# The factors of the norms of a two-layer decoder trunk, moved from ScalarE and VectorE to GpSimd

## The chip, the cores and the metric

The kernel runs on one core of a Trainium2 chip. A core has five engines with a queue of instructions each: TensorE (PE: matrix products and transposes; PEld is its loading of weights), VectorE (DVE), ScalarE (ACT: functions by table, and copies with a scale), GpSimd (POOL) and SyncE (SP, which here issues DMAs). They run side by side and wait for each other by semaphores; each runs its own queue in order. The metric is the device time of one launch in microseconds, the median of several runs.

## The reference, cut to what matters

1024 positions of width 1024 pass two layers. Each layer is a token mixer with four heads of cross attention to a memory of 256 rows, one output projection, and a squared-ReLU MLP of width 4096; layer 0 mixes by latent attention, layer 1 by sliding-window attention. Every branch begins with an RMS norm:

```python
def rmsnorm(x, g):
    y = x * rsqrt(mean(x * x, axis=-1) + EPS)      # EPS = 1e-6
    return y * g

mem_n = rmsnorm(mem, mem_norm_g)
for i in range(2):
    hn = rmsnorm(x, attn_norm_g[i])
    mix, q_cross = mixer_i(hn)                     # layer 0 also norms c_q (384) and c_kv (256)
    x = x + concat(mix, cross(q_cross, mem_n)) @ w_o[i]
    x = x + relu(rmsnorm(x, mlp_norm_g[i]) @ w_up[i])**2 @ w_down[i]
return rmsnorm(x, final_norm_g)
```

What matters here is the factor of each norm, one number per position: the inverse root of the mean square plus EPS.

## The kernel before

**Tiling.** Positions lie on the 128 partitions, in 8 row tiles of 128. A factor is thus a column of 128x1 values, and all arithmetic on it is on such columns (128x2 where two norms share one). Matrix products take each fp32 operand as a high and a low part (`split`: ACT writes the high part, L99 or L102, and DVE subtracts it for the low part, L100 or L103) and run three matmuls (`mm3`, or `mm3w` at L117 to L120). An operand that has to stand with its features on the partitions is transposed by PE into PSUM (`psT...`), and `split` from there.

**Order.** The source is written tile by tile, but the order in which each engine gets its instructions is worked out by the scheduler of the tile framework when the program is built, from the dependencies and from how free each engine is by its reckoning. A change of what runs where thus also changes the order on all engines, and each engine then runs its order as it stands.

**The norms.** There are 50 factors, made in two ways.

- `rstd_of` (L166) and `newton` (L180): ACT squares a tile and sums it (`ss`), DVE turns the sum into mean plus EPS (`z`, L177), ACT takes the root (L184), DVE the reciprocal (L185), and four small DVE operations make a Newton step (L186 to L189). It serves the two memory tiles (`mem_T`; the factor is used at L443, and the product `ym` is transposed at L447), the input norm of each row tile in layer 0 (`norm_y`, used at L206, transposed into `psT_a` at L213), and the two norms on each tile's projection (`a_in`, used at L559 and L560): 18 chains.
- `Rstd.get` (from L1153): the same with one operation fewer (z L1154, root L1155, reciprocal L1156, Newton step L1157 to L1159), for the 32 norms on half rows of 512: the norm ahead of the MLP in `wo_phase` (used by ACT at L1230 and DVE at L1231, transposed into `psT_m` at L1241), and those behind the MLP (`Down.norm` and `late_norm`; used at L1740 or L1694, transposed into `psT_b` at L1751; in layer 1 at L1742 straight to the output).

**Stages.** Memory norm and its projections (to 50 us); layer 0's input projection, one tile each 12.6 us (to 150 us); attention; output projection, whose second half also norms (to 550 us); MLP up and down (to 1175 us); layer 1 likewise (output projection to 1510 us), and the last norm, tile by tile behind the last matmuls. In the projection, the input norm of tile t+1 is made while PE multiplies tile t: `psin` are the projection's sums, `psT_a` the transposes of the next tile's normed input, which stand among them in PE's queue, and `psct` those of the normed result. `psu` and `psv` are products of the MLP's up part, behind the last `psT_m`.

POOL does masks, some products in attention (L430, L2004), the scaling of some weights (L1857) and the issue of some DMAs (L1308, L1688, L1733).

Of the kernel before, what the change touches and what calls it, by code (L numbers as in the profile page):

```python
# [13 lines left out]
AF = mybir.ActivationFunctionType  # L14
ALU = mybir.AluOpType
# [5 lines left out]
D = 1024  # L21
# [5 lines left out]
EPS = 1e-6  # L27
# [28 lines left out]
def trunk(  # L56
# [7 lines left out]
    nc = tc.nc  # L64
# [104 lines left out]
    def rstd_of(pl, src_parts, junk):  # L169

        k = len(src_parts)
        small_ct[0] += 1
        ss = pl.tile([P, 2], F32, tag="ss", bufs=4, name=f"ss{small_ct[0]}")
        z = pl.tile([P, 2], F32, tag="zs", bufs=4, name=f"zs{small_ct[0]}")
        for i, (ap, n) in enumerate(src_parts):
            nc.scalar.activation(junk[:, :n], ap, AF.Square, accum_out=ss[:, i : i + 1])
            nc.vector.tensor_scalar(z[:, i : i + 1], ss[:, i : i + 1], 1.0 / n, EPS, ALU.mult, ALU.add)  # L177
        return newton(pl, ss, z[:, :k], k)

    def newton(pl, ss, z, k):  # L180

        rs = pl.tile([P, 2], F32, tag="rs", bufs=4, name=f"rs{small_ct[0]}")
        rk, t = rs[:, :k], ss[:, :k]
        nc.scalar.activation(t, z, AF.Sqrt)  # L184
        nc.vector.reciprocal(rk, t)  # L185
        nc.vector.tensor_tensor(t, rk, rk, ALU.mult)  # L186
        nc.vector.tensor_tensor(t, t, z, ALU.mult)
        nc.vector.tensor_scalar(t, t, -0.5, 1.5, ALU.mult, ALU.add)
        nc.vector.tensor_tensor(rk, rk, t, ALU.mult)  # L189
        return rs  # L190

    def rstd_halves(pl, xt, junk):

        small_ct[0] += 1
        ss = pl.tile([P, 2], F32, tag="ss", bufs=4, name=f"ss{small_ct[0]}")
        for i, c in enumerate((slice(0, 512), slice(512, 1024))):
            nc.scalar.activation(junk[:, c], xt[:, c], AF.Square, accum_out=ss[:, i : i + 1])
        z = pl.tile([P, 2], F32, tag="zs", bufs=4, name=f"zs{small_ct[0]}")[:, 0:1]
        nc.vector.tensor_scalar(z, ss[:, 0:1], ss[:, 1:2], 1.0 / D, ALU.add, ALU.mult)
        nc.vector.tensor_scalar(z, z, EPS, None, ALU.add)  # L200
        return newton(pl, ss, z, 1)

    def norm_y(pl, xt, y):

        rs = rstd_of(pl, [(xt, D)], y)
        nc.vector.tensor_scalar(y, xt, rs[:, 0:1], None, ALU.mult)  # L206
# [934 lines left out]
    class Rstd:  # L1141
# [9 lines left out]

        def get(self):
            ss, z, rk, t = self.st[:, 0:2], self.st[:, 2:3], self.st[:, 3:4], self.st[:, 4:5]  # L1153
            nc.vector.tensor_scalar(z, ss[:, 0:1], ss[:, 1:2], EPS, ALU.add, ALU.add)  # L1154
            nc.scalar.activation(t, z, AF.Sqrt)  # L1155
# [942 lines left out]
```

## Time and profile before

| | |
|---|---|
| median of three runs | 2132.03 us (2131.01 to 2135.06) |
| profiled execution | 2133.53 us |
| its span, first to last instruction | 2131.8 us |
| mean granted clock of TensorE | 0.998 |
| DVE busy | 1473.0 us, 69% |
| ACT busy | 1136.7 us, 53% |
| POOL busy | 160.0 us, 8% |

1.7 us of the profiled execution lie outside its span. How to read the rows: in the list of waits a row names who waited, for which engine and line, and then the us in total, how often, and the longest. A row of a timeline has start and length in us, engine, line, operation, the written and the read tiles, their shapes, and in brackets how long the engine stood idle just before and for whom. A row of one line's view has its count and the least, median and longest duration in ns. A row of groups has count, busy us and mean ns, then the engine's idle time ahead of it.

### The profile page before, as it was taken

The numbers are of one execution on the slowest core, as the hardware profiler recorded it, in microseconds if no ns is written. First come the engines' busy times: TensorE is split into PE (matmuls) and PEld (weight loads), VectorE is DVE, ScalarE is ACT, GpSimd is POOL, SyncE is SP. The second block draws the span as 40 slices with busy tenths as digits, with TensorE's granted clock in tenths as the row PEclk, the third lists the DMA queues.
The fourth block names the chain that finished last, engine by engine and source line by source line (L and its number), as shares of the span: only waits on it lengthen the run. The fifth ranks groups of instructions, "written<-read, shape, count | busy, mean of one in ns | idle before, by whom it ended". The sixth has DMA issues, their size and how long they took to land.

```text
span 2131.8 us, 29050 instructions
## 1 busy us (share of the span) xinstructions
PE 2081.3 (98%) x9928; PEld 1707.1 (80%) x9928; DVE 1473.0 (69%) x2829; ACT 1136.7 (53%) x2440; POOL 160.0 (8%) x224
## 2 busy tenths in 40 slices
PE   6999999999999999999999999999999999999998
PEld 5888787778777788888888888778888778888887
DVE  7555688865887677886557543866977776976565
ACT  5455477766744544444445553976744443444452
POOL 0012100000000000000001241631000000000000
PEclk9999999999999999999999999999999999999999
DMA  7202223443254455954443211142354446944342
GB/s 255 58 10 56 64 61 81 108 138 108 97 171 144 142 163 184 325 191 140 153 115 94 75 31 50 41 124 80 114 163 163 139 134 222 331 157 155 117 120 88
DMA packets 173726, 275.05 MB, mean 129 GB/s; under 512 B 17189, under 2 KB 72970, under 8 KB 173578
## 3 DMA queue, kind: packets, MB, share of 16 engines
q1 hardware_dynamic: 167008, 256.91, 38.1%
q0 software_dynamic: 4016, 13.12, 1.7%
q10 hardware_dynamic: 2554, 3.17, 0.4%
q8 instruction: 78, 1.28, 0.3%
q14 instruction: 70, 0.57, 0.1%
HBM read 183.79 MB, written 76.86 MB: 122 GB/s over the span
## 4 chain that ended last, share of the span: by engine, by line
PE 75%; DMA 9%; DVE 8%; ACT 5%; issue 2%; SPq 0%; POOL 0%; DVEq 0%; ACTq 0%; POOLq 0%
PE psy L1758 5%; PE psy L1760 5%; PE psy L1759 5%; PE psz L1758 4%; PE psz L1760 4%; PE psz L1759 4%; DMA d<-in_mlp_w_up_dram 4%; PE pss L885 4%; PE pso L927 3%; DMA mr<-in_mlp_w_up_dram 3%; PE psu L1423 3%; PE psu L1425 3%; PE psu L1424 3%; PE pswo L110 2%; PE pswo L108 2%; PE pswo L109 2%
## 5 line engine op out<-in xcount | busy, mean ns | idle before, releaser
L1323 ACT ACTIVATE mr<-mr,gcol 128x256 f32<-128x256 f32 (+1 forms) x160 | 67.2, 477 | 85.1 <-DMA mr<-in_mlp_w_up_dram 81.5
L1323 ACT ACTIVATE d<-d,gcol 128x256 f32<-128x256 f32 x128 | 57.8, 500 | 83.4 <-DMA d<-in_mlp_w_up_dram 76.1
L1758 PE MATMUL psy<-g 128*128 128x512 f32 x256 | 99.9, 390 | 0.0
L1759 PE MATMUL psy<-g 128*128 128x512 f32 x256 | 99.6, 389 | 0.0
L1760 PE MATMUL psy<-g 128*128 128x512 f32 x256 | 99.3, 389 | 0.0
L99 ACT ACTIVATE g<-i 128x512 fp32r<-128x512 f32 x79 | 49.6, 628 | 89.0 <-PE psz L1759 46.4
L100 DVE TENSOR_TENSOR g<-i,g 128x512 fp32r<-128x512 f32 x79 | 55.4, 701 | 49.9 <-ACT g L99 49.7
L99 ACT ACTIVATE uh<-i 128x512 fp32r<-128x512 f32 x66 | 41.6, 630 | 85.3 <-PE psy L1759 40.7
L99 ACT ACTIVATE i<-mr 128x512 fp32r<-128x512 f32 x78 | 49.1, 629 | 69.5 <-PE psy L1759 20.6
L906 ACT ACTIVATE p<-pss 128x512 f32<-128x512 f32 x108 | 63.5, 592 | 41.2 <-PE pss L885 41.1
L100 DVE TENSOR_TENSOR pl<-p,ph 128x512 fp32r<-128x512 f32 (+1 forms) x96 | 61.6, 651 | 27.4 <-ACT ph L99 26.9
L760 DVE TENSOR_REDUCE m<-psx 128x1 f32<-128x128 f32 (+5 forms) x96 | 70.2, 748 | 11.0 <-PE psx L756 10.8
L100 DVE TENSOR_TENSOR uh<-i,uh 128x512 fp32r<-128x512 f32 x66 | 45.5, 690 | 45.3 <-ACT uh L99 45.2
L1759 PE MATMUL psz<-g 128*128 128x512 f32 x192 | 74.7, 389 | 0.0
L1760 PE MATMUL psz<-g 128*128 128x512 f32 x192 | 74.7, 389 | 0.0
L1758 PE MATMUL psz<-g 128*128 128x512 f32 x192 | 74.7, 389 | 0.0
L100 DVE TENSOR_TENSOR i<-mr,i 128x512 fp32r<-128x512 f32 x78 | 53.6, 687 | 22.5 <-ACT i L99 22.2
L99 ACT ACTIVATE ph<-p 128x512 fp32r<-128x512 f32 (+1 forms) x96 | 56.4, 599 | 1.3
L1760 PEld LDWEIGHTS psy<-g 128*128 128x128 f32 x256 | 48.1, 188 | 10.0
L1759 PEld LDWEIGHTS psy<-g 128*128 128x128 f32 x256 | 48.1, 188 | 9.9
L1758 PEld LDWEIGHTS psy<-g 128*128 128x128 f32 x256 | 48.1, 188 | 9.8
L1639 DVE TENSOR_TENSOR mqf<-mqq,mqf 128x512 f32<-128x512 f32 x64 | 43.1, 687 | 16.4 <-DMA mqq<-in_mlp_w_down_dram 16.2
(646 smaller groups left out, 6914.2 us busy)
## 6 DMA issues: line engine op xcount, KB each, us to landing
i<-hd SPq DMA_DIRECT2D x154, 256.0 KB
hd<-uh SPq DMA_DIRECT2D x76, 256.0 KB
hd<-ul SPq DMA_DIRECT2D x76, 256.0 KB
mr<-in_mlp_w_up_dram SPq DMA_DIRECT2D x36, 512.0 KB
hd<-x SPq DMA_DIRECT2D x72, 256.0 KB
mr<-hd SPq DMA_DIRECT2D x70, 256.0 KB
d<-in_mlp_w_up_dram SPq DMA_DIRECT2D x32, 512.0 KB
mqq<-in_mlp_w_down_dram SPq DMA_DIRECT2D x32, 512.0 KB
```

Source lines behind the costliest of these rows:

```text
L99: nc.scalar.activation(hi, src, AF.Copy)
L100: nc.vector.tensor_tensor(lo, src, f32(hi), ALU.subtract)
L760: nc.vector.reduce_max(m8s[h][:, i : i + 1], ps[:, c], axis=AX, negate=True)
L885: return lambda: nc.tensor.matmul(o, a, b, skip_group_check=True, **kw)
L927: mms.append(lambda: nc.tensor.matmul(o, a, b, skip_group_check=True, **kw))
L1323: nc.scalar.activation(w[:, k, :], w[:, k, :], AF.Copy, scale=g_mlp[layer][:, k0 + k : k0 + k + 1])
L1423: nc.tensor.matmul(ps, wh[:, k, :], xh[:, k, :], start=p in (1, 2, 5) and k == 0, stop=False, skip_group_check=True)
L1424: nc.tensor.matmul(ps, wh[:, k, :], xl[:, k, :], start=False, stop=False, skip_group_check=True)
L1425: nc.tensor.matmul(ps, wl[:, k, :], xh[:, k, :], start=False, stop=k == 3, skip_group_check=True)
L1758: nc.tensor.matmul(ps, ah[:, j, :], bh, start=p in (1, 5, 2) and k == 0, stop=False, skip_group_check=True)
L1759: nc.tensor.matmul(ps, ah[:, j, :], bl, start=False, stop=False, skip_group_check=True)
L1760: nc.tensor.matmul(ps, al[:, j, :], bh, start=False, stop=k == NP - 1, skip_group_check=True)
```

## The change

All arithmetic on the factors goes to GpSimd. Root and reciprocal become one power with the exponent -0.5, read from a small constant tile; the Newton step follows with four operations (in `Rstd.get` three before). ScalarE still squares and sums, and still applies factors; its Sqrt goes, and with it the loads of the table that Sqrt needs (eight loads of tables in all before, three now). VectorE loses 281 instructions, ScalarE 62, GpSimd gains 309.

```diff
         for i, (ap, n) in enumerate(src_parts):
             nc.scalar.activation(junk[:, :n], ap, AF.Square, accum_out=ss[:, i : i + 1])
-            nc.vector.tensor_scalar(z[:, i : i + 1], ss[:, i : i + 1], 1.0 / n, EPS, ALU.mult, ALU.add)
+            nc.gpsimd.tensor_scalar(z[:, i : i + 1], ss[:, i : i + 1], 1.0 / n, EPS, ALU.mult, ALU.add)
...
     def newton(pl, ss, z, k):
 
+        G = nc.gpsimd
         rs = pl.tile([P, 2], F32, tag="rs", bufs=4, name=f"rs{small_ct[0]}")
         rk, t = rs[:, :k], ss[:, :k]
-        nc.scalar.activation(t, z, AF.Sqrt)
-        nc.vector.reciprocal(rk, t)
-        nc.vector.tensor_tensor(t, rk, rk, ALU.mult)
-        nc.vector.tensor_tensor(t, t, z, ALU.mult)
-        nc.vector.tensor_scalar(t, t, -0.5, 1.5, ALU.mult, ALU.add)
-        nc.vector.tensor_tensor(rk, rk, t, ALU.mult)
+        G.tensor_tensor(rk, z, mhalf[:, :k], ALU.pow)
+        G.tensor_tensor(t, rk, rk, ALU.mult)
+        G.tensor_tensor(t, t, z, ALU.mult)
+        G.tensor_scalar(t, t, -0.5, 1.5, ALU.mult, ALU.add)
+        G.tensor_tensor(rk, rk, t, ALU.mult)
         return rs
...
     nc.gpsimd.memset(padl, 0.0)
+    mhalf = padl[:, 54:56]
+    nc.gpsimd.memset(mhalf, -0.5)
     nc.gpsimd.memset(padr, 0.0)
...
         def get(self):
             ss, z, rk, t = self.st[:, 0:2], self.st[:, 2:3], self.st[:, 3:4], self.st[:, 4:5]
-            nc.vector.tensor_scalar(z, ss[:, 0:1], ss[:, 1:2], EPS, ALU.add, ALU.add)
-            nc.scalar.activation(t, z, AF.Sqrt)
-            nc.vector.reciprocal(rk, t)
-            nc.vector.scalar_tensor_tensor(t, rk, z, rk, ALU.mult, ALU.mult)
-            nc.vector.tensor_scalar(t, t, -0.5, 1.5, ALU.mult, ALU.add)
-            nc.vector.tensor_tensor(rk, rk, t, ALU.mult)
+            G = nc.gpsimd
+            G.tensor_scalar(z, ss[:, 0:1], ss[:, 1:2], EPS, ALU.add, ALU.add)
+            G.tensor_tensor(rk, z, mhalf[:, 0:1], ALU.pow)
+            G.tensor_tensor(t, rk, rk, ALU.mult)
+            G.tensor_tensor(t, t, z, ALU.mult)
+            G.tensor_scalar(t, t, -0.5, 1.5, ALU.mult, ALU.add)
+            G.tensor_tensor(rk, rk, t, ALU.mult)
             return rk
```

`rstd_halves`, which the diff touches too, is not called. The lines of the changed kernel are two higher than before from L225 on and three higher from L1157 on.

The new order moves instructions on the engines. In layer 0's input projection, PE before, in the tile whose sums are `psin_719`:

```order
L120 MATMUL psin_719<-wih,xhls 128x512
L120 MATMUL psin_719<-wih,xhls 128x416
L117 MATMUL psin_719<-wih,xhls 128x512
L118 MATMUL psin_719<-wil,xhls 128x512
L213 MATMUL psT_a_0_704<-ident,fa_86 128x128 x4
L213 MATMUL psT_a_4_711<-ident,fa_86 128x128 x4
L117 MATMUL psin_719<-wih,xhls 128x416
```

and in the change, where the same tile's sums are `psin_712`:

```order
L120 MATMUL psin_712<-wih,xhls 128x512
L120 MATMUL psin_712<-wih,xhls 128x416
L213 MATMUL psT_a_0_697<-ident,fa_87 128x128 x4
L213 MATMUL psT_a_4_704<-ident,fa_87 128x128 x4
L117 MATMUL psin_712<-wih,xhls 128x512
L118 MATMUL psin_712<-wil,xhls 128x512
```

The transposes of the next tile have moved ahead by eight matmuls of `psin` (two of them are the last two shown ahead of them before). It is so in five of the tiles; in the first one they moved by ten. GpSimd's queue at such a tile, which was empty there but for L305 and L306 (now L307 and L308), holds two chains, of a tile's projection norms (`zs_543`, two factors side by side) and of the next tile's input norm (`zs_566`):

```order
L177 TENSOR_SCALAR zs_543<-ss_542 128x1
L177 TENSOR_SCALAR zs_566<-ss_565 128x1
L177 TENSOR_SCALAR zs_543<-ss_542 128x1
L185 TENSOR_TENSOR rs_548<-zs_543,padl 128x2
L185 TENSOR_TENSOR rs_569<-zs_566,padl 128x1
L186 TENSOR_TENSOR ss_542<-rs_548 128x2
L186 TENSOR_TENSOR ss_565<-rs_569 128x1
L187 TENSOR_TENSOR ss_542<-ss_542,zs_543 128x2
L187 TENSOR_TENSOR ss_565<-ss_565,zs_566 128x1
```

The two chains take turns, through L188 and L189. On VectorE, L559 and L560 (now L561 and L562) wait for the first chain; behind them come the low part of `cT`, the four rope products and one `qc`, and then L206, which needs the second chain.

At the end of layer 0's output projection, ScalarE's queue before, with the norm of the seventh row tile (`d_0_71`):

```order
L1323 ACTIVATE d_0_87_5730<-d_0_87_5730,gcol 128x256 x4
L99 ACTIVATE g_0_95_5798<-x_0_66_5518 128x4x128
L1230 ACTIVATE d_0_71_5566<-i_0_4_4835,cosb 128x512
L99 ACTIVATE g_0_97_5800<-x_0_67_5525 128x4x128
L1323 ACTIVATE d_0_88_5731<-d_0_88_5731,gcol 128x256
L1150 ACTIVATE d_0_73_5621,cosb<-i_0_62_5467 128x512
L1244 ACTIVATE x_0_66_5518<-psT_m_6_0_5631 128x4x128
```

and in the change (`d_0_71` again, with another number behind it):

```order
L1233 ACTIVATE d_0_71_5549<-i_0_4_4818,cosb 128x512
L1326 ACTIVATE d_0_87_5713<-d_0_87_5713,gcol 128x256 x4
L99 ACTIVATE g_0_95_5781<-x_0_66_5501 128x4x128 x2
L99 ACTIVATE g_0_97_5783<-x_0_67_5508 128x4x128
L1247 ACTIVATE x_0_66_5501<-psT_m_6_0_5614 128x4x128
```

The use of the factor (L1230, now L1233) has moved ahead of the four scalings of a weight tile (L1323, now L1326), which wait for that tile's transfer; the copy out of `psT_m` (L1244, now L1247) has stayed behind them.

At the end of layer 0's MLP, GpSimd's queue in the change, with the norms of the fifth (`sinb`) and sixth row tile (`cosb`):

```order
L1691 DMA x_4789<-d_0_156_7968 128x512 x2
L1157 TENSOR_SCALAR sinb<-sinb 128x1
L1157 TENSOR_SCALAR cosb<-cosb 128x1
L1158 TENSOR_TENSOR sinb<-sinb,padl 128x1
L1158 TENSOR_TENSOR cosb<-cosb,padl 128x1
L1159 TENSOR_TENSOR sinb<-sinb 128x1
```

Both chains stand behind two issues of DMAs (L1688 before) and take turns to their ends. At the end of layer 1's output projection PE's order changes as well: the eight transposes of the last row tile into `psT_m` stand behind twelve matmuls of `psu`, where they stood behind 24.

More of the change, by code (lines that the diff above doesn't have):

```diff
@@ L198, in rstd_halves @@
         z = pl.tile([P, 2], F32, tag="zs", bufs=4, name=f"zs{small_ct[0]}")[:, 0:1]
-        nc.vector.tensor_scalar(z, ss[:, 0:1], ss[:, 1:2], 1.0 / D, ALU.add, ALU.mult)
-        nc.vector.tensor_scalar(z, z, EPS, None, ALU.add)
+        nc.gpsimd.tensor_scalar(z, ss[:, 0:1], ss[:, 1:2], 1.0 / D, ALU.add, ALU.mult)
+        nc.gpsimd.tensor_scalar(z, z, EPS, None, ALU.add)
         return newton(pl, ss, z, 1)
```

## The prediction, made before the changed kernel ran

> **What bounds the kernel now.** I read the busy times first, then the list of who waited for whom on PE, then the timeline around each wait.
>
> ```profile
> PE 2081.3 (98%) x9928; PEld 1707.1 (80%) x9928; DVE 1473.0 (69%) x2829; ACT 1136.7 (53%) x2440; POOL 160.0 (8%) x224
> ```
>
> PE is busy for 2081.3 of 2131.8 us. All that can be gained is PE's 50 idle us, and what makes PE idle longer is lost in full. These waits of PE (us in all, times, longest) end on something a norm feeds:
>
> ```profile
> PE psTm L447 <- DVE ss L188: 15.1, 1, 15.1
> PE psT_a L213 <- DVE fa L206: 3.1, 5, 0.7
> ...
> PE psT_m L1241 <- ACT d L1230: 2.2, 2, 2.0
> ...
> PE psu L1423 <- ACT x L1244: 0.9, 1, 0.9
> ```
>
> So the 281 instructions that leave DVE, at 69%, and the Square roots that leave ACT, at 53%, are worth nothing as sums. What counts is how late a factor is at six places: the start, the eight projection tiles (psT_a), the end of layer 0's output projection (psT_m), the end of layer 0's MLP, the end of layer 1's output projection, and the last norm.
>
> **The change, part by part.** Removed from ACT: 50 Sqrts and five loads of function tables.
>
> ```profile
> L184 ACT ACTIVATE ss<-zs x18: 189/203/205, 11.2 to 147.5; 128x1 f32<-128x1 f32 x10, 128x2 f32<-128x2 f32 x8
> L184 ACT ACT_TABLE_LOAD  x2: 1283/1283/1283, 9.5 to 31.4; - x2
> ...
> L1155 ACT ACT_TABLE_LOAD  x2: 1283/1283/1283, 505.2 to 1461.3; - x2
> ```
>
> 50 x 0.2 + 5 x 1.28 = 16.4 us of ACT; the fifth load is one of Exp's two. Only the loads at 9.5 and 31.4 lie on a path to PE. At 505 and 1461 the list of waits has none of PE: the matmuls of the output projection cover them.
>
> Added on POOL: 309 instructions, in chains of six that depend on each other. Their prices (ns: least, median, most):
>
> ```profile
> L1985 POOL COPY sp<-sinks_b x32: 186/190/1187, 1326.4 to 1393.6; 128x3 f32<-128x3 f32 x32
> ```
> ```profile
> L305 POOL TENSOR_TENSOR fa<-fa,ra 128x16 f32<-128x16 f32 x8 | 1.8, 222 | 140.2 <-DVE ra L302 129.8 <-ACT qc L341 10.4
> ...
> L144 POOL TENSOR_SCALAR sinks_b<-sinks_b 128x12 f32<-128x12 f32 x1 | 0.4, 427 | 5.8 <-DMA sinks_b<-in_swa_sinks_dram 5.8
> ```
>
> A multiply of 128x1 I put at d = 0.19, since 128x3 takes 0.190 and 128x16 0.222. The trace has no power on POOL. It is bounded by 0.19 below (it reads and writes as much as a multiply) and by 1.19 above (the longest small instruction on POOL). I take p = 0.43, the longer of the two small arithmetic rows, because a power must cost more than a multiply; both ends stay in the range.
>
> By the Trainium skill (GPSIMD Engine Reference, 4.1 Engine selection) elementwise work belongs on VectorE and two-input work is about twice as slow on GPSIMD. Here 0.19 stands against VectorE's 0.15 for this size; by the page's factor d would be an estimated 0.30, each projection tile would lose 0.8 us more than below, and the sum would end near +10.5, on B's way (below).
>
> *Projection tiles.* One of them, DVE and then PE:
>
> ```profile
> 86.80 0.15 DVE L177 TENSOR_SCALAR zs<-ss 128x1 f32<-128x1 f32 x1 [0.21 <-ACT fa L176]
> ...
> 87.60 0.56 DVE L100 TENSOR_TENSOR cTl<-psct,cTh 128x384 fp32r<-128x384 f32 x1
> 88.07 0.15 DVE L186 TENSOR_TENSOR ss<-rs 128x2 f32<-128x2 f32 x1
> ...
> 89.49 0.62 DVE L559 TENSOR_SCALAR fa<-psin,rs 128x384 f32<-128x384 f32 x1
> 90.02 0.47 DVE L560 TENSOR_SCALAR fa<-psin,rs 128x256 f32<-128x256 f32 x1
> ...
> 92.08 0.75 DVE L206 TENSOR_SCALAR fa<-fa,rs 128x1024 f32<-128x1024 f32 x1
> ```
> ```profile
> 90.49 0.39 PE L117 MATMUL psin<-wih,xhls 128*128 128x512 f32 x1
> ...
> 91.97 0.40 PE L118 MATMUL psin<-wil,xhls 128*128 128x512 f32 x1
> 92.98 1.06 PE L213 MATMUL psT_a<-ident,fa 128*128 128x128 f32 x8 [0.61 <-DVE fa L206]
> ```
>
> PE stood 0.61 us, from 92.37, for L206, which scales the next tile's input. The changed order puts psT_a eight psin matmuls earlier, the stretch from 90.49 to 92.20 (the last of them began at 91.97, 0.23 before the next would): PE now comes at 92.37 - 1.71 = 90.66. On POOL the last z starts at 86.80 as before and ends at 86.99. Two powers, then four steps of each of two interleaved chains; the first factor is done after 2p + 7d = 2.19, at 89.18. DVE, in order, waits there with L559 (87.5 to 89.2 idle but for cTl, which now stands behind L560). Then come L559 0.53, L560 0.5, cTl 0.47 (87.60 to 88.07), four rope products 0.33 and one L342 0.2, so L206 starts at 91.2 and ends at 91.97; PE follows 0.15 later, as it did, at 92.12. Its wait is 1.46 in place of 0.61: +0.85, six times (the order has the pattern before six tiles), **+5.1**. With p = 0.19 it is +0.37 each, +2.2; with p = 1.19 +2.4 each, +14. No DVE work covers it, since DVE itself stands behind the factor.
>
> *Start.* The queues of ACT, POOL and DVE:
>
> ```profile
> 9.34 0.19 ACT L176 ACTIVATION_READ_ACCUMULATOR ym<-mem 128x1 f32 x1
> ```
> ```profile
> 8.68 0.24 POOL L133 MEMSET mask<- 128x128 f32 x1
> 8.86 0.34 POOL L133 MEMSET mask-1_256<- 128x128 f32 x1
> 9.16 0.44 POOL L134 TENSOR_SCALAR_AFFINE_SELECT mask<-mask 128x128 f32<-128x128 f32 x1
> 9.56 0.34 POOL L134 TENSOR_SCALAR_AFFINE_SELECT mask-1_256<-mask-1_256 128x128 f32<-128x128 f32 x1
> ```
> ```profile
> 13.72 1.27 DVE L443 SCALAR_TENSOR_TENSOR ym<-mem,rs,g_mem 128x1024 f32<-128x1024 f32 x1
> ```
>
> The second sum of squares is read by 9.53. In POOL's new order the two chains of the memory rows are interleaved with these four mask instructions: from 9.55 on one z, 1.36 of masks, two powers and seven multiplies up to the first factor, 0.19 + 1.36 + 0.86 + 1.33 = 3.74, so ym starts at 13.3 instead of 13.72: -0.4. The table load at 31.4 also leaves ACT's splits of the input weights, whose transfers end that stage: **-0.5** in all, -1.0 at p = 0.19, +1.1 at 1.19.
>
> *End of layer 0's output projection.*
>
> ```profile
> 546.27 1.71 ACT L1323 ACTIVATE d<-d,gcol 128x256 f32<-128x256 f32 x4 [1.42 <-DMA d<-in_mlp_w_up_dram]
> 547.88 0.61 ACT L99 ACTIVATE g<-x 128x512 fp32r<-128x512 f32 x1
> 548.40 0.71 ACT L1230 ACTIVATE d<-i,cosb 128x512 f32<-128x512 f32 x1
> ...
> 550.55 1.06 ACT L1244 ACTIVATE x<-psT_m 128x512 f32<-128x512 f32 x2
> ```
> ```profile
> 551.17 0.50 PE L1423 MATMUL psu<-mqq,uh 128*128 128x512 f32 x1 [0.92 <-ACT x L1244]
> ```
>
> L1230 now stands ahead of the four L1323 that wait for a transfer, so psT_m no longer stands 1.98 for it. But L1244 stays behind those four and three L99: 547.98 + 3 x 0.53 = 549.6 instead of 550.55. Of the 2.9 us **-1.0** comes back; the transfer is late next.
>
> *End of layer 0's MLP.*
>
> ```profile
> 1171.72 1.14 POOL L1688 DMA_DIRECT2D x<-d x2 [33.26 <-DVE d L1679]
> ```
> ```profile
> 1173.83 0.48 DVE L1694 TENSOR_SCALAR g<-d,sinb 128x512 f32<-128x512 f32 x1
> ```
> ```profile
> 1174.62 0.60 PE L1751 MATMUL psT_b<-ident,g 128*128 128x128 f32 x4
> ```
>
> The factor of the fifth row tile now queues behind two issues of DMAs on POOL, to 1172.86, then runs interleaved with the next chain: two z, two powers, seven multiplies, 0.38 + 0.86 + 1.33 = 2.57, to 1175.43. L1694 takes 0.48 and PE 0.15, 1176.06 in place of 1174.62: **+1.4** (+1.0 at p = 0.19, +3 at 1.19). The other norms of this stage run under matmuls.
>
> *End of layer 1's output projection.*
>
> ```profile
> 1504.43 0.48 PE L1423 MATMUL psu<-mqq,uh 128*128 128x512 f32 x1
> ```
> ```profile
> 1505.29 0.19 ACT L1150 ACTIVATION_READ_ACCUMULATOR d<-i 128x1 f32 x1
> ```
>
> The transposes of the last row tile stood behind 24 such matmuls, at 1510.24. Now they stand behind twelve and are reached at about 1504.43 + 12 x 0.23 = 1507.2. The factor is done at 1505.5 + 5d + p = 1506.9, L1230 takes 0.7 more: PE stands 0.5, where it did not: **+0.5** (0 to +3, since an operation of DVE can hold each POOL step, below).
>
> *Last norm.*
>
> ```profile
> 2125.68 0.21 DVE L1154 TENSOR_SCALAR cosb<-cosb 128x1 f32<-128x1 f32 x1 [0.79 <-ACT i L1150]
> ...
> 2127.00 0.75 DVE L1742 SCALAR_TENSOR_TENSOR i<-i,cosb,mr 128x512 f32<-128x512 f32 x1
> ```
>
> 1.32 us from z to use, nothing beside it. On POOL 5d + p = 1.38 and some 0.03 at each step: **+0.2** (0 to +1).
>
> Sum: 5.1 - 0.5 - 1.0 + 1.4 + 0.5 + 0.2 = **+5.7 us**. The profiled execution took 2133.53, which is 1.5 above the median of the runs: 2139.2 against it, 2137.7 against the median.
>
> **The rivals.**
>
> *A, a power as cheap as a multiply.* With p = 0.19 the terms are +2.2, -1.0, -1.0, +1.0, 0.2 and 0: +1.4, a median near 2133.5, which no measurement tells from no change. For it speaks that a small instruction on POOL has cost 0.2 whatever it did.
>
> *B, POOL is slow or held up.*
>
> ```profile
> 1340.64 1.29 DVE L100 TENSOR_TENSOR woq<-wor,woq 128x1024 fp32r<-128x1024 f32 x1 [0.70 <-ACT woq L99]
> ```
> ```profile
> 1340.79 1.19 POOL L1985 COPY sp<-sinks_b 128x3 f32<-128x3 f32 x1
> ```
>
> A copy that takes 0.19 elsewhere took 1.19 here and ended with DVE's two-input instruction beside it. A power of 1.19, or such holds, give +14, +1.1, -1, +3, +3 and +1: +21, a median near 2153; half way, 2145. Against holds in the projection speaks that DVE waits there. The Trainium skill (GPSIMD Engine Reference, 8 Key points) has the two engines share their SBUF interfaces when VectorE has two SBUF inputs; the pair above agrees.
>
> *C, faster.* The mechanism is the same chain on POOL, in the projection: if the first factor is there by 87.7 instead of 89.18, L206 ends before PE comes at 90.66 and the whole 3.1 us of waits go. With start and psT_m that is 3.1 + 1.3 + 1.0, less 1 at the end of the MLP: -4.4, a median near 2127.6. It decides where z to factor takes below 0.9 us, ten operations of 0.09. The trace has no POOL arithmetic under 0.19, so this is unlikely unless the reordering gains somewhere that I cost at nothing.
>
> That the change fails to do what it says is no case here: in the new order no Sqrt is left on ACT, and three loads of tables.
>
> **How the numbers follow.** About 0.2% (4.3 us) is what a measurement of this kernel can tell from no change, so slower begins at a median of 2136.3, that is at +4.3, and p = 0.36 by these terms. My forecast (p between 0.36 and about 0.7) has 0.38; A and what lies between it and that point 0.37; B 0.15; C 0.10. Slower is forecast and B, 0.53. The range leaves out about a tenth at each end: from 2130, half way between A and C, to 2150, the upper half of B's way.
>
> **What would show it.** POOL's rows at L185 and L1158 give p directly. PE's wait for L206 before psT_a should be near 1.5 us, six times; at 0.6 or less the projection term is wrong, at 2.5 it is B. psTm should start near 14.7. PE should stand about a microsecond at psT_b near 1175 and half of one at psT_m near 1507, and psu of layer 0 should start about a microsecond sooner against its neighbours. I am wrong if the projection's PE waits shrink, or if PE finds new waits in the MLP stages, where I cost POOL's and DVE's meetings at nothing because matmuls lie over them.

## The result, and the profile after

| | before | after |
|---|---|---|
| median of the compared runs | 2131.52 us (2130.66 to 2135.06) | 2160.48 us (2156.76 to 2163.02) |
| ratio | | 1.0137 [1.0125, 1.0150] |
| profiled execution, its span | 2133.53 us, 2131.8 us | 2162.17 us, 2160.5 us |

The kernel became slower by 29 us, five times the 5.7 that were forecast, and above the range. The busy times of after, the line that answers to the first one of the prediction:

```profile
PE 2091.3 (97%) x9928; PEld 1716.4 (79%) x9928; DVE 1434.7 (66%) x2553; ACT 1124.6 (52%) x2385; POOL 249.6 (12%) x533
```

The span grew by 28.7 us. Two parts make it up: PE stands idle for 69.2 us in place of 50.5, 18.7 more; and PE is busy for 2091.3 in place of 2081.3, with the same 9928 matmuls. Those 10.0 us are no work: the same matmuls ran at a lower granted clock (mean 0.991, before 0.998). That share varies from run to run: the four runs have mean clocks of 0.991, 0.991, 0.994 and 0.994, and the two with the higher clock are the two shorter ones. DVE is busy for 38 us less than before and ACT for 12 less, which nothing gained by. The list of who waited for whom, on PE, after (us in all, times, longest):

```profile
PE psTm L449 <- DVE ym L445: 14.6, 1, 14.6
PE psT_a L213 <- DVE fa L206: 11.1, 6, 2.0
PE psT_m L1244 <- ACT d L1233: 5.5, 3, 3.8
PE psu L1426 <- ACT x L1247: 2.5, 1, 2.5
PE pscx L380 <- ACT cps L429: 2.1, 1, 2.1
...
PE psxt L731 <- DVE m L762: 2.0, 1, 2.0
...
PE psT_b L1754 <- DVE g L1697: 1.8, 1, 1.8
```

Against before: psT_a for `fa` 11.1 for 3.1, psT_m 5.5 for 2.2, psu behind `x` 2.5 for 0.9, psT_b new; only the start is shorter, 14.6 for 15.1. (A wait of 2.0 at pscx stood in before too, for another engine: DVE's rb at L304.) To see when the time went, I matched PE's matmuls of both traces by their count from the start and took the difference of their start times. This is a calculation of mine from the timelines (a few rows are missing in each, so it is good to about half a microsecond):

| stage | forecast | lost in the stage, us |
|---|---|---|
| start, to 46 us | -0.5 | -0.9 |
| last memory projections, 46 to 54 us | nothing | +3.0 |
| layer 0's projection tiles | +5.1 | +7.9 |
| start of attention, near 165 us | nothing | +4.5 |
| attention, near 240 us | nothing | +0.7 |
| attention, near 447 us | nothing | +2.1 |
| end of layer 0's output projection | -1.0 | +0.9 |
| end of layer 0's MLP | +1.4 | +3.6 |
| sliding-window attention | nothing | +1 |
| end of layer 1's output projection | +0.5 | +7.0 |
| layer 1's MLP | nothing | -2.9 |
| last norm | +0.2 | +1.6 |

Attention away from these places runs alike in both; layer 1's MLP takes back 2.9. Of the 23 us beyond the forecast about 14 lie at places that the prediction had in its sum, above all at the end of layer 1's output projection, and some 8 at places that it put at nothing.

**What the operations cost.** The power, from the views of its two lines in after (ns: least, median, most):

```profile
L185 POOL TENSOR_TENSOR rs<-zs,padl x18: 534/587/716, 10.0 to 158.1; 128x1 f32<-128x1 f32 x10, 128x2 f32<-128x2 f32 x8
```
```profile
L1158 POOL TENSOR_TENSOR cosb<-cosb,padl x16: 544/562/578, 523.3 to 2153.9; 128x1 f32<-128x1 f32 x16
```

So p is 0.56 on its own, and 0.43 was taken; the eight powers of two columns at L185 took up to 0.72. One whole chain with nothing beside it, the last norm, POOL's timeline and then DVE's:

```profile
2153.47 0.30 POOL L1157 TENSOR_SCALAR cosb<-cosb 128x1 f32<-128x1 f32 x1 [2.91 <-ACT i L1152]
2153.86 0.55 POOL L1158 TENSOR_TENSOR cosb<-cosb,padl 128x1 f32<-128x1 f32 x1
2154.49 0.19 POOL L1159 TENSOR_TENSOR cosb<-cosb 128x1 f32<-128x1 f32 x1
2154.76 0.19 POOL L1160 TENSOR_TENSOR cosb<-cosb 128x1 f32<-128x1 f32 x1
...
```
```profile
2150.60 1.41 DVE L1745 SCALAR_TENSOR_TENSOR d<-d,cosb,mr 128x512 f32<-128x512 f32 x2 [2.93 <-POOL cosb L1162]
2151.93 0.68 DVE L1682 TENSOR_TENSOR i<-psy,i 128x512 f32<-128x512 f32 x1
2155.54 0.75 DVE L1745 SCALAR_TENSOR_TENSOR i<-i,cosb,mr 128x512 f32<-128x512 f32 x1 [2.93 <-POOL cosb L1162]
```

Read the starts, not the durations. A multiply lasts 0.19, as forecast, but one that needs the last one's result starts 0.27 to 0.28 behind it; z with two pointers lasts 0.30. From z to use it is 2.07 us (2153.47 to 2155.54); the forecast had 1.38 and some 0.03 at each step, before had 1.32. The second fence shows how the delay doubles: L1682, which adds the last half row, stands in DVE's queue behind L1745 of the norm before it, which waited 2.93 for POOL. So a late factor makes the next norm start late as well.

**A projection tile**, PE's timeline, to be held against the 0.61 us of before:

```profile
97.88 1.09 PE L213 MATMUL psT_a<-ident,fa 128*128 128x128 f32 x8 [1.88 <-DVE fa L206]
```

**The end of layer 1's output projection**, POOL, DVE and PE in after (rows between left out):

```profile
1523.60 1.06 POOL L1157 TENSOR_SCALAR sinb<-sinb 128x1 f32<-128x1 f32 x1
...
1531.56 0.34 POOL L1157 TENSOR_SCALAR sinb<-sinb 128x1 f32<-128x1 f32 x1
1531.98 0.96 POOL L1158 TENSOR_TENSOR sinb<-sinb,padl 128x1 f32<-128x1 f32 x1
```
```profile
1526.43 0.48 DVE L1234 TENSOR_SCALAR d<-i,sinb 128x512 f32<-128x512 f32 x1 [1.86 <-POOL sinb L1162]
...
1529.84 0.68 DVE L1309 TENSOR_TENSOR i<-pswo,i 128x512 f32<-128x512 f32 x1
...
1534.08 0.49 DVE L1234 TENSOR_SCALAR d<-i,sinb 128x512 f32<-128x512 f32 x1 [1.55 <-POOL sinb L1162]
```
```profile
1530.66 0.39 PE L1428 MATMUL psu<-mqq,ul 128*128 128x512 f32 x1
1534.85 1.97 PE L1244 MATMUL psT_m<-ident,d 128*128 128x128 f32 x8 [3.80 <-ACT d L1233]
...
1537.04 0.63 PE L1427 MATMUL psv<-mqq,uh 128*128 128x512 f32 x1
1537.47 0.63 PE L1428 MATMUL psv<-mqq,ul 128*128 128x512 f32 x1
```

Several things add up. The factor of the seventh tile comes at 1526.4, because POOL's first step took 1.06 instead of 0.30 while DVE ran two-input operations. DVE's L1234 stands 1.86 us for it, and with it all that is queued behind, down to L1309, the last residual add. The new order makes this worse: five two-input operations, 3.0 us, now stand between that use of the factor and the add. In before the add came 0.39 behind the use:

```profile
1503.29 0.48 DVE L1231 TENSOR_SCALAR d<-i,sinb 128x512 f32<-128x512 f32 x1
1503.68 0.68 DVE L1306 TENSOR_TENSOR i<-pswo,i 128x512 f32<-128x512 f32 x1
```

So the eighth tile's norm starts late: z at 1531.56 is 3 us later than in before (1505.51), the 23.0 us lost up to this stage set aside. Its power is held to 0.96 as well, and PE, which now comes here twelve psu sooner, stands 3.80 us. Then PE goes on slowly: psv starts come 0.43 us apart where those of psu came 0.23 apart. The windows of after show why (stretch, its length, busy us and instructions of each engine, then PEclk):

```profile
168.00:172.00 4.00, 2.97 (x15) 2.77 (x14) 1.88 (x3) 2.76 (x12) 3.26 (x2) 0.54 0.02 4
...
448.00:452.00 4.00, 4.00 (x16) 3.26 (x15) 2.17 (x6) 1.79 (x4) 0.00 (x0) 0.57 0.06 11
...
1535.00:1540.00 5.00, 5.00 (x16) 4.26 (x17) 4.47 (x8) 4.54 (x11) 0.00 (x0) 0.50 0.00 0
```

Each of the three stretches follows one of PE's long waits: 2.09 at pscx (and 1.03 at pscT), 2.00 at psxt, 3.80 at psT_m. The granted clock then is 0.50 for 3.4 us (from 448.24 to 451.65) or 6.8 us (from 168.34 to 175.17, and from 1533.67 to 1540.50), and 2 to 3 us are lost on top of the wait. Three more such stretches come near 52, 568 and 1360 us, with waits of 1.68, 2.54 and 2.01 beside them. Before had two, near 552 and 1340 us.

**The ends of layer 0's output projection and MLP**, ACT, DVE and PE in after:

```profile
564.87 0.72 ACT L1233 ACTIVATE d<-i,cosb 128x512 f32<-128x512 f32 x1 [1.80 <-POOL cosb L1162]
565.50 1.69 ACT L1326 ACTIVATE d<-d,gcol 128x256 f32<-128x256 f32 x4
567.10 1.65 ACT L99 ACTIVATE g<-x 128x512 fp32r<-128x512 f32 x3
568.66 0.57 ACT L1247 ACTIVATE x<-psT_m 128x512 f32<-128x512 f32 x1
```
```profile
1194.50 0.49 DVE L1697 TENSOR_SCALAR g<-d,sinb 128x512 f32<-128x512 f32 x1 [3.92 <-POOL sinb L1162]
```
```profile
569.28 0.80 PE L1426 MATMUL psu<-mqq,uh 128*128 128x512 f32 x1 [2.54 <-ACT x L1247]
...
1204.20 0.66 PE L1754 MATMUL psT_b<-ident,d 128*128 128x128 f32 x4 [1.20 <-DVE x L100]
```

L1233 stands ahead of the four L1326 as the new order has it, but for 1.80 us it waits for POOL, and the four, three L99 and L1247 come behind it. PE waits 2.54 for L1247, where it waited 0.92.

### The profile page after: what moved, and what is told of

Same layout as the page of the kernel before. It is cut to its first block, busy times and chain, and to the rows that moved or that the text cites. A ratio compares the mean times of both kernels' runs of the same rounds, so it can differ in the third digit from the quotient of the medians.

```text
span 2160.5 us, 29087 instructions
## 1 busy us (share of the span) xinstructions
PE 2091.3 (97%) x9928; PEld 1716.4 (79%) x9928; DVE 1434.7 (66%) x2553; ACT 1124.6 (52%) x2385; POOL 249.6 (12%) x533
## 3 DMA queue, kind: packets, MB, share of 16 engines
q8 instruction: 78, 1.28, 0.2%
## 4 chain that ended last, share of the span: by engine, by line
PE 53%; DVE 7%; DMA 5%; ACT 4%; issue 3%; POOL 1%; SPq 0%; DVEq 0%; ACTq 0%; POOLq 0%
PE psy L1761 5%; PE psy L1763 5%; PE psy L1762 5%; PE psz L1763 4%; PE psz L1761 4%; PE psz L1762 4%; PE psu L1426 3%; PE psu L1428 3%; PE psu L1427 3%; DMA d<-in_mlp_w_up_dram 2%; DMA mr<-in_mlp_w_up_dram 2%; PE psf L108 2%; PE psf L110 2%; PE psf L109 2%; PE psv L1427 2%
## 5 line engine op out<-in xcount | busy, mean ns | idle before, releaser
L1326 ACT ACTIVATE mr<-mr,gcol 128x256 f32<-128x256 f32 (+1 forms) x160 | 67.2, 477 | 80.7 <-DMA mr<-in_mlp_w_up_dram 66.2
L1326 ACT ACTIVATE d<-d,gcol 128x256 f32<-128x256 f32 x128 | 57.5, 499 | 81.3 <-DMA d<-in_mlp_w_up_dram 56.4
L99 ACT ACTIVATE g<-i 128x512 fp32r<-128x512 f32 x79 | 49.6, 628 | 84.5 <-PE psz L1762 46.2
L99 ACT ACTIVATE uh<-i 128x512 fp32r<-128x512 f32 x66 | 41.6, 631 | 85.6 <-PE psy L1762 40.7
L100 DVE TENSOR_TENSOR g<-i,g 128x512 fp32r<-128x512 f32 x79 | 55.4, 701 | 45.9 <-ACT g L99 45.7
L99 ACT ACTIVATE i<-mr 128x512 fp32r<-128x512 f32 x78 | 49.1, 629 | 70.0 <-PE psz L1762 20.4
L100 DVE TENSOR_TENSOR pl<-p,ph 128x512 fp32r<-128x512 f32 (+1 forms) x96 | 61.6, 652 | 29.7 <-ACT ph L99 29.2
L1157 POOL TENSOR_SCALAR sinb<-sinb 128x1 f32<-128x1 f32 x16 | 7.3, 457 | 604.8 <-ACT d L1152 594.5
L100 DVE TENSOR_TENSOR uh<-i,uh 128x512 fp32r<-128x512 f32 x66 | 45.5, 690 | 43.8 <-ACT uh L99 43.8
L100 DVE TENSOR_TENSOR i<-mr,i 128x512 fp32r<-128x512 f32 x78 | 53.6, 687 | 21.9 <-ACT i L99 21.5
L1860 POOL TENSOR_TENSOR wsr<-wsr,gcol 128x1024 f32<-128x1024 f32 x12 | 23.3, 1944 | 350.3 <-ACT x L99 281.4
L1311 POOL DMA_DIRECT2D xd<-i x32 | 18.9, 591 | 351.5 <-DVE i L1273 288.7
L99 ACT ACTIVATE ph<-p 128x512 fp32r<-128x512 f32 (+1 forms) x96 | 56.4, 599 | 1.3
```

What stands on the lines that cost most here:

```text
L99: nc.scalar.activation(hi, src, AF.Copy)
L100: nc.vector.tensor_tensor(lo, src, f32(hi), ALU.subtract)
L1326: nc.scalar.activation(w[:, k, :], w[:, k, :], AF.Copy, scale=g_mlp[layer][:, k0 + k : k0 + k + 1])
```

## The experiments

Four theories were set against each other at first. The chain: a factor is late by the length of its chain on POOL, and engines that stand for it in order pass that on. The order: the new order of instructions costs by itself. Sharing: POOL is held by DVE. The queue: POOL's chains stand behind the DMAs that POOL issues.

**The power as a multiply, with everything else in place.**

```diff
-    nc.gpsimd.memset(mhalf, -0.5)
+    nc.gpsimd.memset(mhalf, 0.001)
-            G.tensor_tensor(rk, z, mhalf[:, 0:1], ALU.pow)
+            G.tensor_tensor(rk, z, mhalf[:, 0:1], ALU.mult)
```

The same in `newton`.

> The power is replaced by a multiply with 0.001, so the factors are not the reference's; the order of all engines is that of the changed kernel. Theory 1 (latency): the loss is the time from z to factor on GpSimd, 0.56 us of it the power. With 0.19 in its place every single chain is 0.37 us shorter and every pair that takes turns 0.74: six projection tiles -4.4, start -0.7, first tile of attention -0.7, ends of both output projections and of layer 0's MLP -2.5, last norms -0.6, about -9, and some of the stretches of half clock behind long waits go too, up to -4: 2147 to 2152 us. Theory 2 (order): what costs is the order the scheduler chose, which is the same here: 2157 us or more. Theory 3 (the two engines hold each other up at SBUF): also nearly the same, 2156 or more.

Measured: 2144.21 us against 2132.25, ratio 1.0059 [1.0044, 1.0074]. All engines have the order of the changed kernel, so order and sharing alone do not make the 29 us: shortening each chain by 0.37 us (0.56 less 0.19) gave back 16 of them, more than the 9 to 13 expected. PE's waits for the input norm, this kernel:

```profile
PE psT_a L213 <- DVE fa L206: 6.0, 6, 1.1
```

But 12 us stay, where the prediction's rival A, a power as cheap as a multiply, had 1.4. The dear power is not the whole of the error. By matched times 5 us of what stays arise at the end of layer 1's output projection and 3 in the projection tiles.

**The power alone, without the Newton step.**

```diff
         G.tensor_tensor(rk, z, mhalf[:, :k], ALU.pow)
-        G.tensor_tensor(t, rk, rk, ALU.mult)
-        G.tensor_tensor(t, t, z, ALU.mult)
-        G.tensor_scalar(t, t, -0.5, 1.5, ALU.mult, ALU.add)
-        G.tensor_tensor(rk, rk, t, ALU.mult)
```

The same in `Rstd.get`.

> Without the Newton step: z and the power alone, on GpSimd. Theory 1: a chain is 1.0 us instead of 2.1, which is under the 1.3 us that VectorE and ScalarE need together; psT_a finds its input ready in the projection, and the kernel comes out at or under the one before: 2124 to 2134 us. Theory 2: its order on PE is that of the changed kernel but for a few places, so 2150 us or more.

Measured: 2133.79 us against 2132.25, ratio 1.0013 [1.0003, 1.0024]. PE's order differs from the changed kernel's in a few rows of the first tile only (those of DVE and ACT in more places), and PE still comes early to psT_a, but the factor is there:

```profile
PE psT_a L209 <- DVE fa L202: 3.6, 6, 0.7
```

So the work can lie on POOL at almost no loss if the chain is two instructions long. It is no gain: what is won to 70 us, at the end of layer 0's output projection and in layer 1's MLP, 2 to 3 us each by matched times, is lost again at the start of attention (1.6), in sliding-window attention (1.7), at the end of layer 1's output projection (3.1) and in smaller amounts elsewhere. At that last place DVE, in this kernel, still has five operations between the use of the seventh tile's factor and the residual add:

```profile
1501.20 0.49 DVE L1226 TENSOR_SCALAR d<-i,sinb 128x512 f32<-128x512 f32 x1 [0.77 <-POOL sinb L1154]
...
1504.89 0.68 DVE L1301 TENSOR_TENSOR i<-pswo,i 128x512 f32<-128x512 f32 x1
```

PE stands 2.02 at psT_m there, although the chain is shorter than before's. So a part of the loss at this place is not the length of the chain. What is left for it is the order (the add behind five operations, psT_m behind twelve psu) and POOL's first step, which is held to 1.06 here too; no run separates the two.

**One half of the change at a time:** the 18 chains of `newton` on POOL with `Rstd.get` as before, and the other way round.

```diff
         def get(self):
-            G = nc.gpsimd
-            G.tensor_scalar(z, ss[:, 0:1], ss[:, 1:2], EPS, ALU.add, ALU.add)
-            G.tensor_tensor(rk, z, mhalf[:, 0:1], ALU.pow)
...
+            nc.vector.tensor_scalar(z, ss[:, 0:1], ss[:, 1:2], EPS, ALU.add, ALU.add)
+            nc.scalar.activation(t, z, AF.Sqrt)
+            nc.vector.reciprocal(rk, t)
...
```

> Only the 18 factors of newton() on GpSimd (memory norm and layer 0's input projection), the 32 of Rstd.get as before. By the matched times of PE the two kernels are 14.5 us apart at the start of attention, so theory 1 gives 2146 us (2143 to 2149), with half clock near 53 and 170 us as in the changed kernel. If the parts are not additive because the order is shuffled everywhere (theory 2), the 32 other norms also lose time here: 2150 or more.

> Only the 32 factors of Rstd.get on GpSimd, the front as before. Theory 1: what is left of the 28.7 us, 12 to 15, so 2144 to 2147 us, at the ends of both output projections (6 and 1), layer 0's MLP (3.6), the last norm (2). Theory 2: no sum rule; anything up to 2160.

Measured: 2144.77 us (1.0061 [1.0046, 1.0076]) and 2146.66 us (1.0070 [1.0053, 1.0086]), 12.5 and 14.4 us over before. Both lie where the theory of the chain's latency expected them. Together they are 26.9; the whole change cost 29.0 against its own runs of before and 28.2 against these: the halves add. The second half carries as much as the first, where the prediction gave it 1.1 of 5.7.

**DMAs off POOL's queue.** Lines 1311, 1691 and 1736:

```diff
-                    nc.gpsimd.dma_start(out=xd[rows_(t), i * 512 : i * 512 + 512], in_=v_)
+                    nc.sync.dma_start(out=xd[rows_(t), i * 512 : i * 512 + 512], in_=v_)
```

> The changed kernel with the DMAs that POOL issued (lines 1311, 1691 and 1736) issued by SP; PE's order is the changed kernel's. Theory A (POOL's queue): each issue takes 0.64 us of POOL's queue ahead of the z of the same row tile, so at the ends of the output projections the factor comes 0.7 us sooner (three waits at psT_m, -2), at the end of layer 0's MLP 1.2 and 0.7 (-2), with a stretch or two of half clock less (-2 to -4): 2152 to 2157 us. Theory B (the time is in the chain alone, the issues are hidden): 2158 to 2162. Theory C (SP's own queue then holds up loads): slower than the changed kernel, over 2163.

> The power alone everywhere, and no DMA issues on POOL but the first two. By theory A the loss at the end of layer 1's output projection (3 us in the run with the power alone) shrinks by 0.7 to 2: 2130 to 2132.5 us. By B 2133 to 2135 as without the move; by C over 2135.

Measured: 2161.31 against 2131.49, ratio 1.0140 [1.0125, 1.0154]; and with the power alone 2134.10, ratio 1.0014 [1.0004, 1.0023]. In total nothing moved. At the ends of the output projections an issue of 0.64 us runs for the most part while ACT still makes the sum of squares, and PE's longest wait at psT_m stays 3.8. At the end of layer 0's MLP the issues did hold up the fifth tile's factor: without them PE's wait for `g` fell from 1.8 to 0.2. But the sixth tile's chain then no longer took turns with it and came later, and the waits at psT_b for `x` rose from 1.2 to 2.6.

**The power alone in the first half, then with an early load of Exp's table.**

```diff
+        nc.scalar.activation(padl[:, 0:1], cosb[:, 0, 0:1], AF.Exp)
```

This line stands behind the Sin of the rope tables, so that ACT loads Exp's table there and not at the first softmax. The first kernel is the power alone in `newton` with `Rstd.get` as before, the second the changed kernel with this line, the third both together.

> z and power alone on GpSimd for the 18 factors of newton(), no Newton step; the 32 of Rstd.get as before. The run with the power alone everywhere was 2 to 3 us ahead of the kernel before until 70 us and at the end of layer 0's output projection, and lost that in layer 1. Theory 1 keeps the gain: 2128 to 2130.5 us. If the gain was only the removal of table loads, or is lost at the first tile of attention where Exp's table is loaded later: 2131 to 2134.

> The changed kernel with one Exp of a single column behind the Sin of the rope tables, so that Exp's table is loaded there and not at the first tile of attention; PE's order is the changed kernel's. If that load (1.28 us at 162.5) is what PE waits for at pscx: that wait falls from 2.1 to about 0.8, the stretch of half clock behind it goes too, and 2.5 to 4.5 us are won: 2156 to 2158 us. If the late factor of the last projection tile sets it alone: no change, 2159 to 2162.

> The run with the power alone in front (2132.2 us, the kernel before 2131.5) with Exp's table loaded early as in e8. If the load costs the start of attention 1.5 to 3 us there too: 2129 to 2131 us, ahead of the kernel before by a little. If not: 2131.5 to 2133.

Measured: 2132.24 against 2131.49, ratio 1.0001 [0.9992, 1.0010]; 2160.12 against 2130.89, ratio 1.0135 [1.0121, 1.0148]; 2133.12 against 2130.89, ratio 1.0011 [1.0002, 1.0020]. None beats the kernel before. What the early load does at its place is seen all the same. Before, the changed kernel, and the changed kernel with the early load, ACT's and PE's rows:

```profile
149.37 1.28 ACT L427 ACT_TABLE_LOAD   x1
...
152.04 0.38 ACT L561 ACTIVATE fa<-psin 128x256 f32<-128x256 f32 x1 [0.81 <-DVE fa L560]
```
```profile
160.99 0.38 ACT L563 ACTIVATE fa<-psin 128x256 f32<-128x256 f32 x1 [2.21 <-DVE fa L562]
...
162.47 1.28 ACT L429 ACT_TABLE_LOAD   x1
...
167.18 0.38 PE L380 MATMUL pscx<-kmh,qc 128*128 128x256 f32 x1 [2.09 <-ACT cps L429]
```
```profile
169.61 0.39 PE L381 MATMUL pscx<-kmh,qc 128*128 128x256 f32 x1 [0.47 <-ACT cps L430]
```

In before the load stood ahead of L561 in ACT's queue. In the changed kernel it stands behind the same instruction (L563), which waits 2.21 us for DVE and so for the last tile's factor; the first softmax comes 1.28 us later still, and PE stands 2.09 for it. With the early load PE stands 0.47, and the clock, which had fallen to 0.54 and 0.60 in the two stretches from 168 to 176, stays whole in the second of them, as the windows of this kernel show (and in the first, at 1.00 as well):

```profile
172.00:176.00 4.00, 3.90 (x28) 3.90 (x28) 1.51 (x5) 3.02 (x12) 1.94 (x2) 1.00 0.01 4
```

By matched times some 4 us are won there, the half clock included. In the median of four runs they don't appear; in this profile the part ahead of it lost as much, with waits of 5.1 us at psT_a for `vm` (1.7 in the changed kernel) and stretches of half clock. With the power alone in front, the load costs 2 to 3 us at the same place. That the late load costs 2 to 4 us here is shown; that its removal makes the kernel faster is not.

**Work for PE in the long wait.** 24 transposes of the identity, which nobody reads, ahead of the last psT_m of layer 1:

```diff
+                for k in range(24 if layer == 1 and p == 7 and i == 0 else 0):
+                    nc.tensor.transpose(ps[:, 0:P], ident, ident)
```

> The changed kernel with 24 transposes of the identity ahead of the last psT_m of layer 1, into the same PSUM tile, which is then overwritten; they fill 2.5 of the 3.8 us that PE stands there. If a long wait costs twice, once for itself and once in a lower granted clock behind it: the matmuls behind that psT_m run at a spacing of 0.23 instead of 0.43 us, the clock of the 5 us behind it is 1.0 instead of 0.5, and about 2 us are won there (2158 to 2159 in all, hardly more than the runs scatter, so the profile decides). If the low clock has another cause, it stays at 0.5 and nothing is won.

Measured: 2161.67 us, ratio 1.0143 [1.0129, 1.0157], so nothing in total. At the place itself, PE's timeline and a window of this kernel:

```profile
1528.23 2.79 PE L1244 MATMUL psT_m<-ident 128*128 128x128 f32 x24
1532.17 1.09 PE L1246 MATMUL psT_m<-ident,d 128*128 128x128 f32 x8 [1.16 <-ACT d L1233]
...
1533.34 0.40 PE L1429 MATMUL psv<-mqq,uh 128*128 128x512 f32 x1
1533.57 0.40 PE L1430 MATMUL psv<-mqq,ul 128*128 128x512 f32 x1
```
```profile
1535.00:1540.00 5.00, 5.00 (x24) 4.14 (x23) 3.35 (x6) 5.00 (x12) 0.00 (x0) 1.00 0.00 0
```

PE stands 1.16 in place of 3.80, psv runs 0.23 apart, and the clock is 1.00 where it was 0.50. At this place, then, the long wait is what lowers the clock. Between 2 and 3 us were won here. They were lost behind it: the edit also changed the order on ACT and DVE, and from there on psu waited 2.6 us for `x` and 3.5 for `i`, where it had waited 0.4 and 1.7.

**The factor's use moved off DVE.**

```diff
-            nc.vector.tensor_scalar(y[:, 1, :], xb, rs, None, ALU.mult)
+            nc.scalar.activation(y[:, 1, :], xb, AF.Copy, scale=rs)
```

> The changed kernel with the second use of the factor in wo_phase (line 1234) on ACT instead of DVE, so that DVE doesn't stand in its queue for the factor; PE's order is the changed kernel's. Theory (chain plus queue): at the ends of the output projections the residual add of the next row tile (line 1309) then runs when its sum is ready, the next factor is 2 to 4 us earlier, and of the 6 us lost at the end of layer 1's output projection 3 to 5 come back, in layer 0 about 1; ACT has 0.6 us more per row tile: 2153 to 2157 us. If only the chain's own length counts: 2159 or more.

Measured: 2162.38 us, ratio 1.0155 [1.0138, 1.0171]; the theory that DVE's standing is the whole of it fell. DVE no longer waits, but L1309 comes no earlier: it now stands behind a low part (L100) that waits 2.25 for ACT, where L99 is queued behind the moved use. And POOL's chain has become longer, in this kernel:

```profile
1523.09 0.75 POOL L1159 TENSOR_TENSOR sinb<-sinb 128x1 f32<-128x1 f32 x1
1523.92 0.52 POOL L1160 TENSOR_TENSOR sinb<-sinb 128x1 f32<-128x1 f32 x1
1524.52 0.52 POOL L1161 TENSOR_SCALAR sinb<-sinb 128x1 f32<-128x1 f32 x1
```

Steps of 0.19 took 0.52 to 0.75 as soon as DVE had work beside them; z to use became 3.3 us. A DVE that stands for the factor lets POOL run; one that does not stand holds it up.

**A chain of a length in between.** Power with the exponent -1/8, and two squarings.

```diff
-    nc.gpsimd.memset(mhalf, -0.5)
+    nc.gpsimd.memset(mhalf, -0.125)
...
         G.tensor_tensor(t, rk, rk, ALU.mult)
-        G.tensor_tensor(t, t, z, ALU.mult)
-        G.tensor_scalar(t, t, -0.5, 1.5, ALU.mult, ALU.add)
-        G.tensor_tensor(rk, rk, t, ALU.mult)
+        G.tensor_tensor(rk, t, t, ALU.mult)
```

> The power has the exponent -1/8 and two squarings follow it in place of the Newton step, so that the factor comes out of four dependent GpSimd instructions, of which the last starts 0.30 + 0.56 + 0.28 after the first and the use follows at about 1.5 us, between the kernel before (1.32, on VectorE) and the run with the power as a multiply (1.70, which stood 12 us over before). Length theory: the time goes with the length of the chain from z to use, whatever engine makes it: 1.0 us gave +1, 1.70 gave +12, 2.07 gave +28; at 1.5 it gives +4 to +8, a median of 2135 to 2140, and PE's waits at psT_a for the input norm come to 4 to 6 us in all. Engine theory: GpSimd costs by being another engine (its queue, the sharing with VectorE), not by the length, and only the run of the power alone escaped because its queue is half empty: +11 or more, 2142 or above. Threshold theory: PE's waits cost nothing until one of them is long enough for a lower granted clock: 0 to +3, 2131 to 2134.

Measured: 2149.25 against 2131.06, ratio 1.0078 [1.0064, 1.0092]; z to use at the last norm 1.52, as laid out. The length theory's number (2135 to 2140) fell, and so did the threshold's; the engine theory's bound was met, though the power alone, on the same engine, speaks against it. PE's waits for the input norm:

```profile
PE psT_a L211 <- DVE fa L204: 7.5, 6, 1.4
```

That is more than with the power as a multiply (6.0), although a single chain is shorter here (1.52 for 1.70). The reason is visible: in the projection two chains alternate on POOL, where a dependent step of the other one fills the gap and costs 0.15, but each power counts in full. From the last z to L559 (in the changed kernel L561) it is 1.02 us with the power alone, 1.68 with the multiply, 1.99 with the squarings, 2.59 in the changed kernel, and psT_a waits 3.6, 6.0, 7.5 and 11.1. From 1.68 on, six times the added length is what is added to the waits or somewhat less (6 x 0.31 = 1.9 for 1.5; 6 x 0.60 = 3.6 for 3.6). For the total no such line holds: 2149.25 and 2144.21 have intervals that overlap. By matched times the projection tiles and the end of layer 1's output projection cost this run some 5 us each; the rest is spread over the other places of the table.

## Why the prediction was wrong

**Right:** the direction; that the instructions that leave DVE (276 by the busy lines of the two profiles, not 281) and ACT (55, not 62) are worth nothing as sums; the start (psTm at 14.59 for 14.7 forecast); that the projection tiles with PE's earlier psT_a are the largest term, six waits; that the loads of Sqrt's table near 505 and 1461 us bring nothing; that the MLPs cover the meetings of POOL and DVE away from their ends.

**The terms that were mis-sized.** The prediction sized the chains as sums of durations, "5d + p" and "2p + 7d". For a chain by itself that is the step that failed: POOL's dependent steps follow each other at 0.275, not 0.19, z takes 0.30 and the power 0.56, so that z to use is 2.07 and not 1.38. In the projection the sum failed by less. There two chains take turns, the steps go at 0.15, and only the powers were too cheap: 1.18 for the pair where 0.86 was taken. From the end of the last z to L561 it is 2.40 (92.45 to 94.85) for 2.19. What DVE does from there to L206 took 2.2 instead of 2.0, and PE's wait became 1.88 instead of 1.46. Six waits came to 11.1 instead of 8.8. The forecast also took 0.61 as the wait of before at all six, which makes 3.7, where the list of before has 3.1. Together that is +8.0 for +5.1. The two runs with a shorter chain show that most of the total loss hangs on the chain: 16 us went with 0.37 us of each power, all but 1.5 with the Newton step away. The last norm, +1.6 for +0.2, is 0.75 of its own chain and 0.7 of L1682, which stands behind the use of the norm before it.

**The term that had a wrong mechanism.** It is also the one with the largest error. At the end of layer 1's output projection the prediction took the factor as done "at 1505.5 + 5d + p", from the time of before at which the sum of squares was read. That time itself moved by 3 us: DVE stood for the seventh tile's factor with the residual add of the eighth behind it, and the new order had put five operations between the two. So the eighth tile got the delay twice, with POOL held by DVE in both chains. PE's wait came to 3.80 instead of 0.5, the seventh tile's transposes waited 0.85 instead of 0.22, and the half clock added 2 to 3 us: +0.5 became +7.0, more than twice the upper end of that term. With the power alone 3.1 us of it stayed, so that the length of the chain is not all of it. At the end of layer 0's output projection a factor's use holds up what is behind it as well: the prediction had L1244 at 549.6 instead of 550.55 because L1230 would no longer be behind the four weight scalings; it stood ahead of them for 1.80 us and held them up, +0.9 for -1.0. At the end of layer 0's MLP, +3.6 for +1.4, L1697 stood 3.92 and PE waited 1.80, and again 1.20 for the next tile's low part queued behind. The prediction named what is queued behind a wait in the projection; here it did not. The run with the use on ACT moves the standing to ACT and lengthens the chain, and wins nothing.

**What was not costed.** First, the clock: 10.0 us of the 28.7 are PE running slower, of which 8.3 went with the cheap power (PE busy 2083.0 there). That a long wait brings it on is shown at one place by the filled wait; for the others it is argued from the same picture (wait, then half a clock) and was not tried. Second, the start of attention, +4.5: the Exp load, counted as a saving because one of two is gone, moved in ACT's order behind an instruction that waits for the last tile's factor, so that it lies where PE waits. With the early load that stage cost 0.3. Third, 3 us at 46 to 54 us and smaller ones in attention; the waits at psT_a near 50 us vary (2.7 us in all in the changed kernel, 3.5 with the issues moved, 5.1 with the early load, all with one order on PE), and the cause of these losses stays open.

**The rivals.** B, POOL slow or held, came nearest, with 2145 to 2153, but for the reason it named only in part. The sum of its terms was short above all by the clock, the start of attention and the doubled delay. A fell: the cheap power cost 12 us, not 1.4. C had the right variable: its point was a chain below 0.9 us, and the power alone at 0.97 (2126.10 to 2127.07 at the last norm) reached no loss worth the name, but no gain either.

## What to carry to other kernels

Price a chain of small dependent operations by the distance of their starts on the engine that will run them, not by their durations, and look for an alternating partner that fills the gaps. Where an engine comes to stand for a result, list what is behind it in its queue: if the next round's input is among it, the delay counts twice, and a new order can put more work between the two. An idle engine is no reason to move latency-bound work to it; here 38 us less work on DVE were worth nothing, and chains that are longer by some 0.75 us came, with what they brought on, to 29.

## What the runs showed of the hardware

- A power on POOL takes 0.56 us for 128x1; the nearest rows of before were 0.22 and 0.43. A dependent multiply there lasts 0.19 but its successor starts 0.27 to 0.28 after it; with two independent chains in turns a step starts every 0.15.
- POOL's 128x1 steps took 0.52 to 1.06 us instead of 0.19 to 0.56 with two-input DVE operations beside them.
- The granted TensorE clock fell to 0.50 for 3.4 or 6.8 us after waits of PE of 2.00, 2.09 (with 1.03 close behind) and 3.80 us. The length of a wait does not settle it. After the waits of 1.88 in the projection the clock stayed whole in the profiled execution of the changed kernel, but it fell after one of 1.87 there in the run with the chains of `newton` alone on POOL (96.1 us) and after one of 1.95 in the run with the filled wait (81.6 us). At layer 1's psT_m it fell after 2.02 with the power alone and did not after 2.04 with the issues moved as well. The Trainium skill (TensorE: Matmul & The Clock Gate, HAM oscillation — how this bites in real kernels) gives as a rule "no PE-idle gaps >~3.4µs". The wait of 3.80 agrees; at those of 2.0 PE was also partly idle in the microseconds around (2.0 of 4 us busy from 444 to 448), so a single gap of 3.4 us was not needed here.
